# Moving the pooling mixer's PSUM bank to the pool of the wide products, and three empty steps in attention's turn, in a two-layer hybrid decoder trunk

## The chip, the cores and the metric

The kernel runs on one core of a Trainium2 chip, in float32 throughout; large matrix products are done with operands split into a high and a low part. The metric is the time of one execution on the device in microseconds, given as a median over runs.

## The reference

Two layers work on 256 positions of width 1024. In each layer, in this order:

```
h += 0.5 * SwiGLU(RMSNorm(h))                      # width 2816
u  = RMSNorm(h); one input projection of u, split into
     A) sparse attention: an indexer of 8 heads picks the 64 best keys of each query,
        8 heads attend to them through a latent of rank 256
     B) pooling mixer: means over trailing windows of 2, 4, 8, 16 minus the input,
        a 128x128 map for each of the 4 groups, a scale for each channel
     C) Mamba-2 state space: causal convolution, chunked scan in 2 chunks of 128,
        16 heads of 64 in 2 groups, SiLU gate, norm
     and three sigmoid gates
h += W_out( sum over branches of sigmoid(gate) * Lift(branch) )
h += 0.5 * SwiGLU(RMSNorm(h))
h += sigmoid(RMSNorm(h) W_g) * (p W_p)
```

A final RMSNorm follows the last layer. The change lies in the middle part, where A, B and C run beside one another.

## The kernel before, in words

**Products.** Activations lie transposed, 128 channels on the partitions and 256 positions along the free axis. A weight unit of 128x1024 is loaded, split by ScalarE into `whi` (line 140) and by VectorE into `wlo` (line 141), and used as the stationary operand. `mm3` (line 163) makes one product out of three: high by high (line 166), high by low (167), low by high (168). One pair of projection columns is 2 units x 8 blocks x 3 = 48 such products into one PSUM bank. They are called wide here: they use the whole 128x128 array.

**Narrow products.** Some products use half the array. Scores and indexer products have 64 contracted rows (`products`, line 684). Attention's values (`values`, line 765) and the state-space products within a chunk (`near`, line 927) have 64 output columns, one head. All of these go through `mm` (line 105), so all have line 106 in the profile; their tiles tell them apart: `aux<-ki,a` indexer, `aux<-a,a` scores, `aux<-t,a` values, `aux<-ct,ul` state space. Values and `near` are plain float32 and show two rows for a product.

**Banks.** PSUM is handed out by `bank` (line 92) from two pools of four banks: `mm` for the wide products, and `aux` for all that is small: narrow products, transposes (line 109), the state-space helpers and, at line 999, the pooling mixer's product.

**The weave.** After the projections that attention and the state space need, four generators run in turn (`weave`, line 645, called at line 602): `states` (the state space, weight 56), `attend` (attention, 34), `pools` (pooling, 24) and `gate` (the gate projections, 43). Each `yield` ends a step; the generator with the smallest share of steps done goes next. A step of `gate`, or of the projections in `pools`, issues 12 wide products. `states` and `attend` are `apart`: when one of them yields a function, it is parked until the other yields one too, and then the two functions are called one behind the other. So four times a layer a *round* is traced: `near` of one group and chunk, then attention's next products. The rounds are `near` with the scores of the first 128 queries; `near` with their values and the scores of four heads of the other queries; `near` with those values and the last scores; `near` with the last values.

**Order on TensorE.** The program is first traced and then ordered for each engine by a list scheduler that works with estimated times: an instruction traced earlier goes first among those that it takes to be ready. `mm` and `transpose` pin each of their instructions behind the TensorE instruction traced just before it; `mm3` doesn't, so wide products fill in wherever a narrow one isn't taken to be ready. The order on each engine is thus fixed when the kernel is built.

**Attention's chain.** `softmax` (line 731) masks and reduces each score on VectorE (line 744), takes the exponential on ScalarE (line 746), scales (line 750), transposes with TensorE (line 758) and copies out with ScalarE (line 761). It yields twice in the first part, three times to wait, and once behind each of two sets of transposes. `attention` (line 777) then yields once, and then hands over the function with the values.

**The pooling chain.** `pool_group` (line 975) copies its input out of PSUM (line 981), builds the window sums, splits the result (lines 185 and 186), and issues one `mm3` into the bank of line 999, which `split_scaled` (lines 189 and 190) reads.

Of the kernel before, what the change touches and what calls it, by code (L numbers as in the profile page):

```python
# [64 lines left out]
class Builder:  # L65
# [711 lines left out]
    def attention(self, mb, q, kt, vt, ya):  # L777


        two, pair, py = [], [], []  # L780

        def scores(h, g):
            two[:] = self.products(g, 4 // (h + 1), slice(h * P, (h + 1) * P), (h + 1) * P, q,
                                   lambda y, c: kt[y][:, c])

        def out(h):
            if not py:
                py.append(self.bank("aux"))
            self.values(h, py[0], pair, vt)
            pair.clear()  # L790

        def done(h):
            qs = slice(h * P, (h + 1) * P)
            self.split(ya[:, 0, :, qs], ya[:, 1, :, qs],
                       py.pop().rearrange("p (a b) -> p a b", a=4))

        yield lambda: scores(0, 0)
        yield from self.softmax(0, two, mb[0], pair)
        yield
        yield lambda: (out(0), scores(1, 0))  # L800
        done(0)
        yield from self.softmax(1, two, mb[1], pair)
        yield
        yield lambda: (out(1), scores(1, 2))
        yield from self.softmax(1, two, mb[1], pair)
        yield
        yield lambda: out(1)
        done(1)
# [166 lines left out]
    def pool_group(self, layer, g, ps, wpl, yp):  # L975
        nc = self.nc
        w = WINDOWS[g]
        pad = 16
        x = self.t([P, pad + S + 16], tag="t1")[:, :pad + S]
        nc.vector.memset(x[:, :pad], 0.0)  # L980
        nc.scalar.copy(x[:, pad:], ps)
        cur, have = x, 1
        while have < w:
            n = self.t([P, pad + S + 16], tag="t1")[:, :pad + S]
            nc.vector.tensor_copy(n[:, :have], cur[:, :have])
            nc.vector.tensor_tensor(n[:, have:], cur[:, have:], cur[:, :pad + S - have], op=OP.add)
            cur, have = n, 2 * have
        yield

        nc.vector.tensor_tensor(cur[:, pad:pad + 16], cur[:, pad:pad + 16],  # L990
                                self.col(layer, "pool_corr", g * 16, 16), op=OP.mult)
        y = self.t([P, S], tag="t1")
        nc.vector.scalar_tensor_tensor(y, cur[:, pad:], 1.0 / w, x[:, pad:],
                                       op0=OP.mult, op1=OP.subtract)
        yh = self.t([P, S], FR, tag="t1")
        yl = self.t([P, S], FR, tag="t1")
        self.split(yh, yl, y)
        yield
        po = self.bank("aux")
        s = slice(g * P, (g + 1) * P)  # L1000
        self.mm3(po[:, :S], (wpl[0][:, s], wpl[1][:, s]), (yh, yl), True, True)
        self.split_scaled(yp[:, 0, g], yp[:, 1, g], po[:, :S], self.col(layer, "pool_scale", g))
# [211 lines left out]
```

## Time and profile before

| what | value |
|---|---|
| median of 3 runs | 1325.61 us (1325.14 to 1326.77) |
| the profiled execution | 1326.89 us |
| its span, first to last instruction | 1325.2 us |
| mean granted clock of TensorE | 0.996 |
| layer 0: indexer, then the four rounds | 231.65, 259.18; 321.84, 337.97, 364.50, 381.80 us |
| layer 0: first product of the lift | 388.50 us |

PE is TensorE's products, PEld its loads of the stationary operand, DVE VectorE, ACT ScalarE. A row of the timeline gives the start and the duration in microseconds, the engine, the line, the operation, the tiles written and read, the part of the array used (rows*columns), the shape, and how many instructions the row merges. Products overlap: each takes about 0.28 us from its start to its modelled end, while the next one starts after about 0.11 us. What a product costs is therefore the distance between starts, and not its duration.

### The profile page before, as it was taken

The page shows a single profiled execution, that of the slowest core. Times are in us where ns is not written, and L with a number is a line of the kernel's source. Part 1 is how long each engine was busy: PE and PEld are TensorE (multiplying, and loading weights), DVE is VectorE, ACT ScalarE, POOL GpSimd, SP SyncE. Part 2 cuts the span into 40 slices and gives each one's busy share as a digit, 9 for nine tenths or more (in the row PEclk, how much of TensorE's full clock was granted, in tenths as well). Part 3 has the DMA queues.
Part 4 walks back from the last instruction along what each step waited for, and adds up shares of the span by engine and source line. Part 5 has one row for each costly group of instructions (what it writes and reads, how often), then busy time and mean ns, then how long its engine had stood idle before and what let it go on. Part 6 is the DMA issues. An engine that isn't in the chain of part 4 may idle for free.

```text
span 1325.2 us, 28279 instructions
## 1 busy us (share of the span) xinstructions
PE 1306.6 (99%) x11502; PEld 1296.1 (98%) x11502; DVE 1039.6 (78%) x1971; ACT 740.9 (56%) x1209; POOL 7.0 (1%) x17
## 2 busy tenths in 40 slices
PE   7999999999999999999999999999999999999997
PEld 7999999999999999999999999999999999999997
DVE  6877659987989787766887776699789888777666
ACT  5554446756864555444655444566577546544454
POOL 0000000000000000000000000000000000000000
PEclk9999999999999999999999999999999999999998
DMA  7666655567546566666656666556665466666661
GB/s 260 193 193 195 197 176 183 184 187 212 167 144 206 185 208 193 194 198 193 188 180 195 196 196 189 159 191 191 195 195 163 144 215 210 195 197 194 192 193 47
DMA packets 72385, 248.24 MB, mean 187 GB/s; under 512 B 7936, under 2 KB 10304, under 8 KB 72256
## 3 DMA queue, kind: packets, MB, share of 16 engines
q1 hardware_dynamic: 71392, 245.17, 60.2%
q8 instruction: 90, 1.47, 0.5%
q10 hardware_dynamic: 864, 1.28, 0.3%
q14 instruction: 39, 0.32, 0.1%
HBM read 245.33 MB, written 1.08 MB: 186 GB/s over the span
## 4 chain that ended last, share of the span: by engine, by line
PE 97%; DVE 1%; ACT 1%; DMA 0%; issue 0%; DVEq 0%; ACTq 0%
PE mm L166 30%; PE mm L168 30%; PE mm L167 30%; PE aux L106 3%; PE aux L167 1%; PE aux L168 1%; PE aux L166 1%; PE aux L109 1%; DMA h<-in_x_dram 0%; DVE wlo L141 0%; DVE acc L225 0%; ACT whi L140 0%; DVE ul L190 0%; ACT uh L189 0%; DVE h L1031 0%
## 5 line engine op out<-in xcount | busy, mean ns | idle before, releaser
L140 ACT CAST whi<-raw 128x1024 fp32r<-128x1024 f32 (+1 forms) x457 | 476.0, 1045 | 491.4 <-issue 229.1
L166 PE MATMUL mm<-uh,whi 128*128 128x256 f32 x2550 | 706.5, 279 | 7.2 <-ACT whi L160 6.7
L168 PE MATMUL mm<-uh,wlo 128*128 128x256 f32 x2560 | 708.9, 278 | 1.8 <-DVE wlo L141 1.8
L167 PE MATMUL mm<-ul,whi 128*128 128x256 f32 x2560 | 707.8, 277 | 0.0
L141 DVE TENSOR_TENSOR wlo<-raw,whi 128x1024 fp32r<-128x1024 f32 (+1 forms) x457 | 551.7, 1213 | 195.0 <-ACT whi L140 193.7
L166 PEld LDWEIGHTS mm<-uh,whi 128*128 128x128 f32 x2550 | 478.9, 188 | 9.8 <-ACT whi L160 6.7
L168 PEld LDWEIGHTS mm<-uh,wlo 128*128 128x128 f32 x2560 | 481.8, 188 | 3.0 <-DVE wlo L141 2.4
L167 PEld LDWEIGHTS mm<-ul,whi 128*128 128x128 f32 x2560 | 482.1, 188 | 0.2 <-DVE ul L190 0.2
L168 PE MATMUL mm<-gh,wlo 128*128 128x256 f32 x704 | 194.1, 276 | 0.0
L167 PE MATMUL mm<-gl,whi 128*128 128x256 f32 x704 | 194.1, 276 | 0.0
L166 PE MATMUL mm<-gh,whi 128*128 128x256 f32 x704 | 193.7, 276 | 0.0
L168 PEld LDWEIGHTS mm<-gh,wlo 128*128 128x128 f32 x704 | 132.2, 188 | 0.0
L167 PEld LDWEIGHTS mm<-gl,whi 128*128 128x128 f32 x704 | 132.2, 188 | 0.0
L166 PEld LDWEIGHTS mm<-gh,whi 128*128 128x128 f32 x704 | 131.9, 188 | 0.0
L167 PE MATMUL mm<-a,whi 128*128 128x256 f32 x256 | 70.3, 276 | 0.0
L166 PE MATMUL mm<-a,whi 128*128 128x256 f32 x256 | 70.2, 276 | 0.0
L168 PE MATMUL mm<-a,wlo 128*128 128x256 f32 x256 | 69.9, 277 | 0.0
L166 PEld LDWEIGHTS mm<-a,whi 128*128 128x128 f32 x256 | 47.9, 188 | 0.0
L167 PEld LDWEIGHTS mm<-a,whi 128*128 128x128 f32 x256 | 47.9, 188 | 0.0
L168 PEld LDWEIGHTS mm<-a,wlo 128*128 128x128 f32 x256 | 47.6, 188 | 0.0
L373 DVE TENSOR_TENSOR t<-mm,rs_r 128x256 f32<-128x256 f32 x88 | 37.2, 423 | 9.8 <-PE mm L168 0.6
L378 DVE SCALAR_TENSOR_TENSOR t<-t,t 128x256 f32<-128x256 f32 x88 | 37.4, 425 | 3.0
(215 smaller groups left out, 1105.7 us busy)
## 6 DMA issues: line engine op xcount, KB each, us to landing
raw<-in_w_dram SPq DMA_DIRECT2D x447, 512.0 KB, 4.3
gh<-rates SPq DMA_DIRECT2D x16, 256.0 KB, 4.3
raw<-in_w_dram SPq DMA_DIRECT2D x8, 352.0 KB, 3.0
raw<-in_w_dram SPq DMA_DIRECT2D x4, 256.0 KB, 3.7
gh<-rates SPq DMA_DIRECT2D x8, 128.0 KB, 3.4
h<-in_x_dram SPq DMA_DIRECT2D x2, 256.0 KB, 4.2
h<-in_x_dram SPq DMA_DIRECT2D x1, 512.0 KB, 5.7
t<-in_p_dram ACTq DMA_DIRECT2D x2, 256.0 KB, 5.9
```

The costliest lines, as they stand in the source:

```text
L106: self.tc.keep_in_program_order(self.nc.tensor.matmul(*args, **kw))
L109: self.tc.keep_in_program_order(self.nc.tensor.transpose(*args))
L140: nc.scalar.copy(hi[:, :n], raw[:, :n])
L141: ins = nc.vector.tensor_tensor(lo[:, :n], raw[:, :n], hi[:, :n].bitcast(F), op=OP.subtract)
L166: (self.mm if keep else mm)(ps, a[0], b[0], start=start, stop=False)
L167: mm(ps, a[0], b[1], start=False, stop=False)
L168: mm(ps, a[1], b[0], start=False, stop=stop)
L373: nc.vector.tensor_tensor(t, p1[0], r, op=OP.mult)
L378: nc.vector.scalar_tensor_tensor(g, th, 1.0, t, op0=OP.add, op1=OP.mult)
```

## The change

In `pool_group`, line 999, the bank for the product of each pooling group comes from the pool of the wide products. In `attention`, the generator yields once more ahead of each of the three functions that hold values (behind lines 799, 803 and 806). Nothing else differs: the same instructions, transfers and weight units. Every layer runs line 999 four times.

```
         yield lambda: scores(0, 0)
         yield from self.softmax(0, two, mb[0], pair)
         yield
+        yield
         yield lambda: (out(0), scores(1, 0))
         done(0)
         yield from self.softmax(1, two, mb[1], pair)
         yield
+        yield
         yield lambda: (out(1), scores(1, 2))
         yield from self.softmax(1, two, mb[1], pair)
+        yield
         yield
         yield lambda: out(1)
         done(1)
...
         yield
-        po = self.bank("aux")
+        po = self.bank()
         s = slice(g * P, (g + 1) * P)
         self.mm3(po[:, :S], (wpl[0][:, s], wpl[1][:, s]), (yh, yl), True, True)
```

In a few words it was described as one state-space bank from the pool of the wide products, and attention steps once more ahead of its values, so that narrow products lie in six runs a layer.

More of the change, by code (lines that the diff above doesn't have):

```diff
@@ L799, in attention @@
         yield
+        yield
         yield lambda: (out(0), scores(1, 0))
@@ L803, in attention @@
         yield
+        yield
         yield lambda: (out(1), scores(1, 2))
         yield from self.softmax(1, two, mb[1], pair)
+        yield
         yield
@@ L998, in pool_group @@
         yield
-        po = self.bank("aux")
+        po = self.bank()
         s = slice(g * P, (g + 1) * P)
```

## The prediction

> **What bounds the kernel now.** I read the page first, then who made TensorE wait, then the busy time of the stretch that the change touches, and last the order of TensorE's instructions in that stretch. From the page:
>
> ```profile
> span 1325.2 us, 28279 instructions
> PE 1306.6 (99%) x11502; PEld 1296.1 (98%) x11502; DVE 1039.6 (78%) x1971; ACT 740.9 (56%) x1209; POOL 7.0 (1%) x17
> PE 97%; DVE 1%; ACT 1%; DMA 0%; issue 0%; DVEq 0%; ACTq 0%
> ```
>
> The second line is busy time by engine, the third the chain that ended last. Both say TensorE. Its longest wait in the answer on waits is at the very start, and the busy time of 190 to 388 us, which holds all of layer 0's woven stretch, leaves it almost no gap:
>
> ```profile
> PE mm L166 <- ACT whi L160: 6.7, 1, 6.7
> 190.00:388.00 198.00, 197.79 (x1758) 193.23 (x1757) 172.58 (x389) 132.49 (x248) 2.37 (x2) 1.00 0.60 183
> ```
>
> TensorE is busy for 197.79 of 198.00 us there, at a granted clock of 1.00. So the change cannot gain by removing a wait of TensorE, for there is none; it can gain only if the same products take less of TensorE's time, and it loses by any wait that it puts in.
>
> How much time a product takes depends on its neighbours. Ordinary products use the whole array (128*128 in the rows). Narrow ones use half: 64 rows for scores, 64 columns for the state-space products and the attention values. The rows below are TensorE's timeline of layer 0 in order of start: start, duration, then the form and how many products the row merges. First the two runs of the indexer, with the wide products around one of them:
>
> ```profile
> 231.44 0.28 PE L168 MATMUL mm<-uh,wlo 128*128 128x256 f32 x1
> 231.65 1.55 PE L106 MATMUL aux<-ki,a 64*128 64x128 f32 x24
> 233.13 0.39 PE L166 MATMUL mm<-uh,whi 128*128 128x256 f32 x1
> 233.36 0.28 PE L167 MATMUL mm<-ul,whi 128*128 128x256 f32 x1
> ...
> 259.18 1.70 PE L106 MATMUL aux<-ki,a 64*128 64x256 f32 x24
> ```
>
> Then the four rounds in which the state-space products (ct,ul), the values (t,a) and the scores (a,a) are traced together:
>
> ```profile
> 321.84 1.09 PE L106 MATMUL aux<-ct,ul 128*64 128x128 f32 x16
> ...
> 337.97 0.65 PE L106 MATMUL aux<-ct,ul 128*64 128x128 f32 x6
> ...
> 338.98 0.87 PE L106 MATMUL aux<-ct,ul 128*64 128x128 f32 x10
> ...
> 340.12 0.28 PE L168 MATMUL mm<-uh,wlo 128*128 128x256 f32 x1
> 340.33 0.43 PE L106 MATMUL aux<-t,a 128*64 128x128 f32 x2
> 340.69 0.39 PE L166 MATMUL mm<-uh,whi 128*128 128x256 f32 x1
> 340.91 0.28 PE L167 MATMUL mm<-ul,whi 128*128 128x256 f32 x1
> 341.03 0.28 PE L168 MATMUL mm<-uh,wlo 128*128 128x256 f32 x1
> ...
> 342.30 1.09 PE L106 MATMUL aux<-t,a 128*64 128x128 f32 x14
> 343.31 0.38 PE L106 MATMUL aux<-a,a 64*128 64x256 f32 x1
> ...
> 344.69 0.28 PE L168 MATMUL mm<-uh,wlo 128*128 128x256 f32 x1
> 344.90 0.97 PE L106 MATMUL aux<-a,a 64*128 64x256 f32 x11
> 345.80 0.39 PE L166 MATMUL mm<-uh,whi 128*128 128x256 f32 x1
> 346.02 0.28 PE L167 MATMUL mm<-ul,whi 128*128 128x256 f32 x1
> ...
> 364.50 1.09 PE L106 MATMUL aux<-ct,ul 128*64 128x128 f32 x16
> 365.42 0.60 PE L106 MATMUL aux<-t,a 128*64 128x128 f32 x4
> ...
> 367.56 1.09 PE L106 MATMUL aux<-t,a 128*64 128x128 f32 x12
> ...
> 369.32 0.97 PE L106 MATMUL aux<-a,a 64*128 64x256 f32 x11
> ...
> 381.80 1.09 PE L106 MATMUL aux<-ct,ul 128*64 128x128 f32 x16
> 382.73 1.09 PE L106 MATMUL aux<-t,a 128*64 128x128 f32 x16
> ```
>
> Count the runs, a run being narrow products with no whole-array product between them. Indexer: two. Round one, at 321.84: one. Round two is torn into five (6 state-space products; 10 more; 2 values; 14 values and 1 score; 11 scores). Round three is torn into three (16 and 4; 12 and the first score; 11 scores). Round four: one. That is 12 a layer. Layer 1 is cut in the same places, as its row of 14 values shows:
>
> ```profile
> 993.28 1.09 PE L106 MATMUL aux<-t,a 128*64 128x128 f32 x14
> ```
>
> Six runs a layer would be the two of the indexer and one for each round, so the change says that it joins the five pieces of round two and the three of round three.
>
> **What one run costs.** Between two whole-array products of ordinary pace lies 0.12 us (340.91 to 341.03); 16 narrow ones take 0.92 us (364.50 to 365.42), 0.0575 each. The run of two at 340.33: from the wide product before it (340.12) to the second after it (340.91) pass 0.79 us. Two wide steps are 0.24 and two narrow ones 0.115, which leaves 0.435 us for going in and coming out. The run of 11 scores: from 344.69 to 346.02 pass 1.33 us, less 0.24 and 11 x 0.0575 = 0.63, leaves 0.46. The long indexer run: from 231.44 to 233.36 pass 1.92, less 0.24 and 24 x 0.0575 = 1.38, leaves 0.30. The two short runs are of the kind that would vanish, so I take 0.44 us and keep 0.30 and 0.46 as ends. The switch shows on both sides: 0.21 us from a wide product to the first narrow one, 0.22 between the first two wide ones after a run, where 0.12 is normal.
>
> The Trainium skill, TensorEngine Tiling (Array Packing), Key Properties, says that changing the tiling mode, and not merely the tile, drains TensorE. The trace agrees in kind: 0.435 and 0.46 us for a way in and a way out. The skill's TensorE: Matmul & The Clock Gate, Single matmul latency, puts a drain at about 175 ns; two of them, an estimate from that page, would be 0.35 us a run and 4.2 us for twelve.
>
> **The change part by part.** No instruction is added or taken away, no transfer, no weight unit; the order of the weight units stays too. What changes is which PSUM bank four small products a layer write, and where attention's steps fall between the others.
>
> *The bank (line 999).* The pooling mixer's product no longer takes one of the four "aux" banks, which near-products, values, scores and transposes share. In round two its product started at 337.76, straight before the state-space products at 337.97. With its bank, the state-space bank, the values' bank and the first score bank live, the four are full and the second score bank has to wait; by my reading that is why one score product runs at 343.31 and 11 follow only at 344.90. Round three ends in the same way, with 11 scores apart at 369.32. Without that tenant these two tears go. It also lets attention's transposes pass: in round three the second set is traced directly behind a pooling product and pinned to it. With the extra steps it is traced behind a gate product instead, though the first set then comes behind the pooling product.
>
> *The extra steps (after lines 799, 803, 806).* They hold the values back so that the softmax, the transposes and their copies are done when a round begins. Two values at 340.33 and 14 at 342.30 are parted by such a copy:
>
> ```profile
> 339.42 0.59 ACT L761 COPY t<-aux 128x512 f32<-128x512 f32 x1
> ```
>
> It ends at 340.01, and two values are already out at 340.33 with the first copy. Counting the code's steps, round two comes to stand behind no further wide product, rounds three and four each behind 24 more than now. Delay for the state-space branch, which waits parked for attention, is covered by those same gate products, so I cost it at nothing. If that cover were gone, the end would feel it: attention's result is ready at 385.17 and the lift begins at 388.50, so 3.3 us of cover are to spare, while 24 products less are 24 x 0.12 = 2.9 us.
>
> ```profile
> 384.48 0.69 DVE L186 TENSOR_TENSOR a<-aux,a 128x512 fp32r<-128x512 f32 x1 [0.72 <-ACT a L185]
> ...
> 388.50 0.28 PE L166 MATMUL mm<-a,whi 128*128 128x256 f32 x1
> ```
>
> *Sum.* Six runs fewer a layer, two layers: 12 x 0.44 = 5.3 us less on TensorE (ends 12 x 0.30 = 3.6 and 12 x 0.46 = 5.5). TensorE is the bound, so all of it comes off the end. The profiled execution took 1326.89 us, 1.7 more than its span and 1.3 above the median 1325.61; against it the sum is 1321.6, against the median 1320.3. The likeliest case's own range is 1319.5 to 1322.5: the two ends, with half a microsecond for the spread of the runs.
>
> **Rivals.** *Some tears stay.* Round two gets no wide product more ahead of it, and the copy at 339.42 still comes after the state-space products could start; values may again go out in two parts. If only the tears made by banks go, two to four runs a layer vanish: 4 x 0.44 = 1.8 to 8 x 0.44 = 3.5 us, 1322.1 to 1323.8. For it speaks that the tear between 2 and 14 values follows the copy and no bank.
>
> *The wide pool is asked in order, and TensorE stands.* This one ends slower. Banks of a pool seem to be granted in the order of the code: the state-space products of round two had their factors early (the multiply of line 922 ended at 330.38) and yet began only after the pooling product at 337.76, which asks for a bank before them. If the pool of the wide products does the same, the next pair of projections cannot start until the pooling product has its input:
>
> ```profile
> 329.09 1.29 DVE L922 TENSOR_TENSOR ct<-ct,gl 128x512 f32<-128x512 f32 x2
> ...
> 336.28 0.40 ACT L185 CAST t<-t 128x256 fp32r<-128x256 f32 x1
> ...
> 337.76 0.28 PE L166 MATMUL aux<-t,whi 128*128 128x256 f32 x1
> ...
> 359.37 0.41 ACT L185 CAST t<-t 128x256 fp32r<-128x256 f32 x1
> ...
> 362.26 0.28 PE L166 MATMUL aux<-t,whi 128*128 128x256 f32 x1
> ```
>
> The second pooling product stands in the code 48 wide products behind round one, and 24 more need no new bank. Round one begins at 321.84 and has 16 and 24 narrow products, 40 x 0.0575 = 2.3 us, so the 72 wide ones start at about 324.3 and are done 72 x 0.12 = 8.6 us later, at 332.9. The input is ready at 336.68, so TensorE would stand about 3.7 us. For the third pooling product the code's steps put 45 wide products fewer ahead of it than the trace has: 362.26 - 45 x 0.12 = 356.9, with the input ready at 359.78: 2.9 us, unless the first wait has swallowed it. Against 2.64 us saved by whole runs that is 1.1 to 4.0 us lost a layer: 1327.7 to 1333.5, say 1330.5. It decides wherever the pooling input comes later than the last product that has a bank already. Against it: the weave keeps two pairs going, and four banks hold both, one being emptied and one more. The Trainium skill, Perfetto Trace Analysis, Identifying Performance Opportunities, says that repeated gaps on the engine that should be full can mean too little PSUM for the next tile; here no such gap stands in the rows, and by that rule they would appear with the fifth tenant.
>
> *The change does not do what its words say*, and the order of the products stays as it is: 1325.6. The words speak of a state-space bank, while line 999 is the pooling mixer's; round two's unmoved place in the code speaks for a little of this, the two tears that a bank makes against it.
>
> **How the numbers follow.** A measurement of this kernel can tell about 0.2%, 2.65 us, from no change. Whole runs (1320.3) get 0.52, tears in part (1322.1 to 1323.8, half of it beyond 0.2%) 0.22, nothing 0.08, the standing TensorE 0.18. Faster: 0.52 + 0.11 = 0.63; within 0.2%: 0.11 + 0.08 = 0.19; slower 0.18. I name the likeliest, 1320.3. The range goes from 1319.5, under the full gain, to 1329.5, which takes in the smaller half of the slower case; what lies outside is about 0.14.
>
> **What would show it.** Right: TensorE's timeline has one narrow run in each round of both layers, no idle time before a pooling product, and the stretch from the first indexer run to the lift is 2.6 us shorter a layer, with all other stages as long as now. Tears in part: runs counted between 7 and 11. The standing TensorE: idle time on TensorE in the woven stretch, released by ScalarE's cast of line 185 or a release of a wide bank, where now there are 0.21 us. Wrong altogether: six runs and the stretch no shorter, which would mean that a run costs less than its neighbours' spacing says.

## The result, and the profile after

| kernel | median of 4 runs | lowest to highest | profiled execution | its span |
|---|---|---|---|---|
| before | 1325.41 us | 1325.14 to 1326.77 | 1326.89 us | 1325.2 us |
| after | 1339.47 us | 1338.98 to 1340.77 | 1339.73 us | 1338.0 us |

The change makes the kernel slower: the ratio is 1.0103, with a 95% interval of 1.0091 to 1.0116, or 14.1 us. The forecast was 1320.3 us. (The profiled execution of before lies 1.5 us above its median, so the two profiles differ by 12.8 us in span.)

The page of the changed kernel, its span, its busy times and its chain:

```profile
span 1338.0 us, 28291 instructions
...
PE 1306.5 (98%) x11502; PEld 1296.9 (97%) x11502; DVE 1044.9 (78%) x1971; ACT 741.8 (55%) x1209; POOL 7.0 (1%) x17
...
PE 90%; DVE 5%; ACT 3%; issue 1%; DMA 1%; DVEq 0%; SPq 0%; ACTq 0%
```

TensorE is busy for 1306.5 us, against 1306.6 before, with the same 11502 products. The span is 12.8 us longer, so TensorE idles 1338.0 - 1306.5 = 31.5 us where it idled 18.6: 12.9 us more. The chain says the same in another way: TensorE's share fell from 97% to 90%, and VectorE and ScalarE now hold 8% of it. The answer on waits names the place (the columns are: us in total, times, the longest):

```profile
PE mm L166 <- ACT t L185: 10.9, 4, 4.8
PE mm L166 <- ACT whi L160: 6.8, 1, 6.8
PE aux L109 <- ACT t L750: 2.1, 2, 1.0
```

The first and the third line are new: 10.9 + 2.1 = 13.0 us, the whole growth of the idle time. Line 166 with the bank `mm` and an input from the cast of line 185 is the pooling product, which waits for its input. Now TensorE's timeline of layer 0, from before round two to the end of round three (a bracket gives the idle time before the row and what ended it):

```profile
327.07 0.39 PE L166 MATMUL mm<-t,whi 128*128 128x256 f32 x1 [0.62 <-ACT t L185]
...
333.00 0.60 PE L109 MATMUL aux<-ident,t 128*128 128x128 f32 x4
334.64 1.21 PE L109 MATMUL aux<-ident,t 128*128 128x128 f32 x4 [1.04 <-ACT t L750]
335.81 0.39 PE L166 MATMUL mm<-t,whi 128*128 128x256 f32 x1
...
338.90 0.28 PE L168 MATMUL mm<-uh,wlo 128*128 128x256 f32 x1
339.11 1.09 PE L106 MATMUL aux<-ct,ul 128*64 128x128 f32 x16
340.03 1.04 PE L106 MATMUL aux<-t,a 128*64 128x128 f32 x16
341.01 0.98 PE L106 MATMUL aux<-a,a 64*128 64x256 f32 x12
341.92 0.39 PE L166 MATMUL mm<-uh,whi 128*128 128x256 f32 x1
342.14 0.28 PE L167 MATMUL mm<-ul,whi 128*128 128x256 f32 x1
...
356.49 0.28 PE L168 MATMUL mm<-uh,wlo 128*128 128x256 f32 x1
361.59 0.58 PE L166 MATMUL mm<-t,whi 128*128 128x256 f32 x1 [4.83 <-ACT t L185]
361.97 0.41 PE L166 MATMUL mm<-uh,whi 128*128 128x256 f32 x1
362.19 0.41 PE L167 MATMUL mm<-ul,whi 128*128 128x256 f32 x1
...
370.38 1.09 PE L106 MATMUL aux<-ct,ul 128*64 128x128 f32 x16
371.31 1.09 PE L106 MATMUL aux<-t,a 128*64 128x128 f32 x16
372.33 0.98 PE L106 MATMUL aux<-a,a 64*128 64x256 f32 x12
```

Three things are to be seen. First, the narrow products lie as the change's words say, in six runs a layer, though the bank that moved is the pooling mixer's and not one of the state space: rounds two and three are one run each (16 state-space products, 16 values, 12 scores, with no wide product between), and the two layers together have 12 runs where they had 24. From 338.90 to 342.14 pass 3.24 us, less two wide steps of 0.12 leaves 3.0 for the whole of round two, and 3.1 for round three. The five and three pieces of before, measured in the same way, took 4.9 and 4.2 us. (Round three of before stands directly behind four transposes, whose own steps are not counted; here are the rows ahead of it.)

```profile
363.85 0.28 PE L168 MATMUL aux<-t,wlo 128*128 128x256 f32 x1
363.97 0.60 PE L109 MATMUL aux<-ident,t 128*128 128x128 f32 x4
```

That saves 3.1 us a layer, 0.52 for each run that vanished.

Second, TensorE stands before the pooling products: 0.62 us before the first; 2.81 us (333.00 to 335.81) with only eight transposes in them before the second; 4.83 us before the third. The next pair of projections, which had its inputs, follows each time only behind the pooling product. Third, the wide products behind the longest wait start 0.21 us apart (361.97 to 362.19 and on) and not 0.12. The busy times of that wait and of the stretch behind it show why; the number behind PE, PEld, DVE, ACT and POOL is the granted clock:

```profile
356.00:361.60 5.60, 0.77 (x8) 0.57 (x7) 5.13 (x13) 2.90 (x7) 0.00 (x0) 0.94 0.62 200
361.60:366.40 4.80, 4.80 (x22) 4.80 (x23) 3.48 (x13) 0.62 (x2) 0.00 (x0) 0.50 0.35 119
```

The granted clock is 0.50 over these 4.80 us, in which 22 products start; at the step of 0.113 us that wide products have elsewhere, 42 would. None of this counts as idle time, and so it hides in the busy time that did not fall. From 361.97, 21 products take 4.48 us instead of 21 x 0.113 = 2.4, a loss of 2.1 us; in layer 1, where the same wait of 4.83 us stands, the same 21 lose 1.4 us. In layer 0 the clock is still low behind them: the next two wide products and eight transposes take 1.65 us, and in layer 1, with the clock back, 1.03, which is 0.6 us more.

The account of the two layers: +13.0 us idle (6.49 in each), +4.1 at half clock, some +1.7 around the transposes (2.81 us a layer, less 1.04 that counts as idle and 8 x 0.115, the step of a wide product, for the transposes), -6.2 for whole runs: +12.6 us. From the first indexer product to the lift, layer 0 grew from 156.85 to 164.32 us and layer 1 from 156.79 to 162.96, 13.6 us together. (That is more than the 12.8 us between the spans, because the profiled execution of before reached its first indexer product 0.9 us later.) The remaining 1.0 us I did not place.

### The profile page after: what moved, and what is told of

Its sections match the earlier page's. It is cut to its first block, busy times and chain, and to the rows that moved or that the text cites. A ratio compares the mean times of both kernels' runs of the same rounds, so it can differ in the third digit from the quotient of the medians.

```text
span 1338.0 us, 28291 instructions
## 1 busy us (share of the span) xinstructions
PE 1306.5 (98%) x11502; PEld 1296.9 (97%) x11502; DVE 1044.9 (78%) x1971; ACT 741.8 (55%) x1209; POOL 7.0 (1%) x17
## 4 chain that ended last, share of the span: by engine, by line
PE 90%; DVE 5%; ACT 3%; issue 1%; DMA 1%; DVEq 0%; SPq 0%; ACTq 0%
PE mm L166 28%; PE mm L168 28%; PE mm L167 28%; PE aux L106 2%; DVE wlo L141 2%; ACT whi L140 1%; PE aux L109 1%; ACT t L746 1%; PE aux L167 1%; DVE ct L919 1%; PE aux L168 1%; PE aux L166 1%; DVE acc L225 0%; DMA h<-in_x_dram 0%; DMA raw<-in_w_dram 0%
```

## The experiments

The first theory, A: the banks of a pool are granted in the order of the code, so that a pooling product that asks the pool `mm` for a bank and has no input yet holds up every later pair of projections, ready or not. Theory B: the extra steps make attention late, and its banks and results hold up the rest. Theory C: the pool `mm` has too few banks with a fifth tenant. Each experiment was timed in five rounds beside the kernel before, on the same chip (medians of before 1325.45 for the first four, 1325.44 for the others). Runs are counted in TensorE's timeline, over both layers; idle is the span less TensorE's busy time.

| kernel | runs | idle, us | median, us | ratio (95%) |
|---|---|---|---|---|
| before | 24 | 18.6 | 1325.4 | |
| after | 12 | 31.5 | 1339.47 | 1.0103 (1.0091 to 1.0116) |
| bank alone | 16 | 30.4 | 1341.13 | 1.0115 (1.0101 to 1.0129) |
| steps alone | 26 | 18.2 | 1327.95 | 1.0019 (1.0010 to 1.0028) |
| early first write | 34 | 18.6 | 1329.94 | 1.0034 (1.0021 to 1.0046) |
| indexer torn | 36 | 18.9 | 1331.29 | 1.0047 (1.0033 to 1.0061) |
| wait filled | 14 | 21.2 | 1337.18 | 1.0086 (1.0072 to 1.0100) |
| input's bank, more steps | 12 | 19.9 | 1321.39 | 0.9971 (0.9961 to 0.9982) |
| input's bank, three steps | 22 | 19.8 | 1326.75 | 1.0009 (1.0000 to 1.0018) |
| asked one step later | 16 | 24.5 | 1327.65 | 1.0016 (1.0007 to 1.0025) |

### The bank alone, and the steps alone

The change's two halves, one by one. The bank alone:

```
-        po = self.bank("aux")
+        po = self.bank()
```

> The bank of line 999 from the wide pool, without the extra steps. Its order on TensorE has 16 narrow runs in all (24 before, 12 after). Theory A (the wide pool grants its banks in the order of the code, so the next pair of projections stands behind a pooling product whose input is late): the waits for the cast of line 185 stay, one of 4 to 5 us and one of about 0.6 us a layer, and the time is 1338 to 1342 us. Theory B (the extra steps make attention and the parked state-space branch late): no such wait, and 8 runs fewer than before at 0.58 us each, 1321 us. Theory C (too few wide banks, whatever the order of asking): as A.

The steps alone:

```
         yield from self.softmax(0, two, mb[0], pair)
         yield
+        yield
         yield lambda: (out(0), scores(1, 0))
...
         yield
+        yield
         yield lambda: (out(1), scores(1, 2))
         yield from self.softmax(1, two, mb[1], pair)
+        yield
         yield
         yield lambda: out(1)
```

> The three extra steps, with the pooling product in the small pool as before. 26 narrow runs. Theory A and theory C: TensorE has no wait in the woven stretch, and two runs more than before cost about 1 us: 1326 to 1327 us. Theory B: waits of several us a layer, about 1339 us.

The bank alone took 1341.13 us, 15.7 more than before, and TensorE's waits are those of the changed kernel:

```profile
PE mm L166 <- ACT t L185: 9.9, 4, 4.3
PE mm L166 <- ACT whi L160: 6.6, 1, 6.6
PE aux L109 <- ACT t L750: 2.0, 2, 1.1
```

The steps alone took 1327.95 us, 2.5 more, with no wait on a cast of line 185 in its answer on waits. So the loss belongs to the bank, and B falls. The steps by themselves do not make the runs whole either: there are 26, two more than before.

### An early first write

The changed kernel, with one product more into each pooling bank, in a half that nothing reads, whose operands are there long before. Its result is not used. The bank is asked for at the same place and kept as long; only its first write no longer waits for the pooling input.

```
         po = self.bank()
+        nc.tensor.matmul(po[:, S:], self.onesr, wpl[0][:, :S], start=True, stop=True)
```

> The changed kernel with one more product for each pooling group, whose result nobody reads: it writes the unused half of the group's bank from operands that are ready early, so that the bank is asked for and granted at once. Eight products more in all (1 us), 34 narrow runs. Theory A: the waits for the cast of line 185 go, since the next pair no longer stands behind the late input; 10 runs more than before cost about 5 us and the products 1 us: 1330 to 1332 us. Theory B: the waits stay, 1339 us or more. Theory C: the waits stay too, since the bank is held longer than in the changed kernel: 1339 us or more.

It took 1329.94 us, 9.5 less than the changed kernel, with eight products more. All that its answer on TensorE's waits holds:

```profile
PE mm L166 <- ACT whi L160: 6.3, 1, 6.3
PE mm L168 <- DVE wlo L141: 1.3, 3, 0.9
PE mm L166 <- ACT whi L140: 1.1, 1, 1.1
PE aux L106 <- DVE acc L225: 1.0, 1, 1.0
PE aux L106 <- ACT t L223: 0.8, 1, 0.8
```

The waits for line 185 and for the transposes are gone, with the same four banks and the same five tenants. Too few banks cannot be the cause, and C falls; what held TensorE up was the order in which the banks are first written. The prediction's sentence from the Trainium skill, Perfetto Trace Analysis, Identifying Performance Opportunities, that such gaps can mean too little PSUM, named a sign that came, but not its cause here. A second finding came unasked: without the wait there are 34 runs. So the changed kernel's whole runs seem to be owed in part to the standing itself: with nothing wide ready, nothing could come between. (Every edit here also lets the list scheduler order TensorE anew, so no run changes the banks and nothing else.)

### The indexer torn

What a run costs: the kernel before, with the two runs of the indexer in each layer cut into eight, and the four rounds as they were.

```
-        self.weave((choose(), 26), (silus(), 60), (some(12), 12))
+        self.weave((choose(), 34), (silus(), 60), (some(12), 12))
...
+    def product_steps(self, g, per, qs, nk, q, key, sides):
+        sides += [(self.bank("aux"), *self.heads(g + i, per)) for i in range(2)]
         for j in range(per):
             for x, y in ((0, 0), (1, 0), (0, 1)):
...
+            yield
...
+        all_sides = []
+        for g in range(0, 8 // per, 2):
+            yield from self.product_steps(g, per, qs, nk, qi, lambda y, c: ki[y], all_sides)
```

> The kernel before, with the indexer's two runs a layer cut into eight by a step after each six products; everything else in TensorE's order is as before, with 36 runs instead of 24. It prices a run by itself. At the 0.44 us of the prediction 12 more runs give 1330.7 us; at the 0.30 us of the long indexer run 1329.0; at the 0.58 us by which rounds two and three became shorter in the changed kernel, 1332.4; if only neighbours shift and nothing is lost, 1325.4.

It took 1331.29 us, 5.84 more. But the edit does more than the expectation says. For the second 128 queries `product_steps` is called twice with the same growing list, so its second call issues the products of the first call again: 12 more a layer, 24 in all. TensorE's count shows them (11526 against 11502), and so do the indexer's runs, of which two in each layer have 12 products and not 6:

```profile
PE 1310.6 (99%) x11526; PEld 1297.4 (98%) x11526; DVE 1039.7 (78%) x1971; ACT 741.4 (56%) x1209; POOL 3.4 (0%) x17
263.06 0.98 PE L106 MATMUL aux<-ki,a 64*128 64x256 f32 x12
```

A run of 24 such products takes 1.70 us in the kernel before (at 259.18), a run of 12 here 0.98, so one costs 0.060 us and the 24 cost, as an estimate, 1.4 us. That leaves 4.4 us for 12 runs more, 0.37 us a run. The early first write bears this out: 10 runs more and eight wide products (0.9 us), with as much idle time as before, cost 4.5 us, which is 0.36 a run. The 0.58 us in the expectation counted transposes of the kernel before as part of round three; it should be the 0.52 us above.

### The wait filled

The changed kernel, with 48 products more in each layer ahead of the third pooling product, into an `aux` bank that nothing reads. It asks what the half clock costs.

```
+        if g == 2:
+            pd = self.bank("aux")
+            for _ in range(48):
+                nc.tensor.matmul(pd[:, :S], self.onesr, wpl[0][:, :S], start=True, stop=True)
         po = self.bank()
```

> The changed kernel with 48 products more a layer, whose results nobody reads, in a bank of the small pool just ahead of the third pooling product: TensorE has them to do where it now waits 4.83 us. 48 x 0.113 = 5.4 us of work fills the wait; 14 narrow runs instead of 12. If the halved granted clock behind that wait comes from the wait, it stays at 1.00 and the 2.1 + 0.7 us of layer 0 and the 1.4 us of layer 1 that the slow products cost are won back: 1339.5 - 4.2 + 0.8 (work longer than the wait) + 1.0 (two runs) = 1337 us, with 96 products more. If the clock falls for another reason, 1341 us.

With 96 products more the kernel took 1337.18 us, 2.3 less than the changed one. The same moment of layer 0, its busy times with the granted clock as above:

```profile
358.00:362.00 4.00, 4.00 (x36) 4.00 (x35) 3.41 (x13) 0.77 (x3) 0.00 (x0) 1.00 0.64 205
362.00:366.00 4.00, 4.00 (x37) 4.00 (x37) 3.04 (x8) 3.19 (x7) 0.00 (x0) 1.00 0.18 24
```

The clock stays at 1.00, and there is no wait of 4.8 us left. So the half clock follows from the wait, and its price comes on top of it.

### Asked one step later

The changed kernel, with one more step between the split of the pooling input and the asking for the bank:

```
         self.split(yh, yl, y)
         yield
+        yield
         po = self.bank()
```

> The changed kernel with one step more in the pooling group between the split of its input and the asking for the wide bank. 16 narrow runs. Theory A: the third product is asked for after round three, when its input has long been ready, so the wait of 4.83 us and the halved clock go; the small waits in round two may stay (0.6 us and the transposes in a block, some 3 us a layer): 1325.4 - 8 x 0.49 + 2 x (1 to 3) = 1323.5 to 1327.5 us. Theory C (number of banks, not the order): about 1339 us.

It took 1327.65 us, 11.8 less than the changed kernel, with the same bank from the same pool. Its waits:

```profile
PE mm L166 <- ACT t L185: 3.5, 4, 1.1
...
PE aux L109 <- ACT t L750: 2.1, 2, 1.0
```

The wait for line 185 went from 10.9 to 3.5 us, though only the place of the asking in the code moved. The sum comes near: 8 runs fewer than before are 8 x 0.37 = 3.0 us saved, and 24.5 - 18.6 = 5.9 us more idle; +2.9, and +2.2 were measured.

### The bank of its own input

If the order of asking is the trouble, a pooling product that asks for no bank has none. Here it is written into the half bank from which its own input was copied, which it holds anyway:

```
-        po = self.bank("aux")
         s = slice(g * P, (g + 1) * P)
-        self.mm3(po[:, :S], (wpl[0][:, s], wpl[1][:, s]), (yh, yl), True, True)
+        self.mm3(ps, (wpl[0][:, s], wpl[1][:, s]), (yh, yl), True, True)
```

with the read by `split_scaled` changed likewise. One kernel has the change's three steps. In the other there are two extra ahead of the first values, four ahead of the second and none ahead of the third, chosen so that the order on TensorE has six runs a layer.

> The pooling product in its input's bank, and just the three extra steps of the change. 22 narrow runs. Theory A: no wait, two runs fewer than before: 1324.5 us. The difference to the changed kernel, about 15 us, is then due to the bank alone. Theory B: about 1339 us.

> The pooling product goes into the half bank from which its own input was copied out, so it asks for no bank at all; two extra steps ahead of the first values, four ahead of the second, none ahead of the third. 12 narrow runs, as in the changed kernel. Theory A: no wait of TensorE in the woven stretch, and 12 runs fewer at the 0.49 us of the torn indexer give 1319.6 us (1318.4 at 0.58). Theory B (late values cost the time): six extra steps a layer, slower than the changed kernel's three, over 1339 us. Theory C (too few wide banks): the input's bank is held longer, some waits, 1325 us or more.

With the change's steps it took 1326.75 us, with no wait for line 185 on a pooling product, and 22 runs. Against the changed kernel that is 12.7 us less, with the same steps and ten runs more: the bank's price, net of the runs that it made whole. With the other steps it took 1321.39 us, 4.05 less than the kernel before (interval of the ratio 0.9961 to 0.9982), the only version faster than both. Its waits:

```profile
PE mm L168 <- DVE wlo L141: 1.8, 5, 0.9
...
PE mm L166 <- ACT t L185: 0.9, 2, 0.5
```

It has the 12 runs that the change was described with, and 1.3 us more idle than before. 12 x 0.37 = 4.4 saved, less 1.3, makes 3.1; 4.05 were measured. The expectations, 1319.6 and 1324.5 us, were each some 2 us too low: they left out these small waits, and the first counted 12 runs at 0.49 us.

The input's bank with three steps, with two runs fewer and 1.2 us more idle, should be +0.5 and is +1.3. For these two and the kernel that asks later, the sum of runs and idle time is thus right to about 1 us. For the steps alone it is not: they should cost 2 x 0.37 - 0.4 = 0.3 us and cost 2.5. What the rest is stays open.

## Why the prediction was wrong

**What bounds the kernel: right.** TensorE was full, and a change could lose by any wait that it puts in. That happened.

**The whole runs: right in number and near in price, but in part by luck.** Six runs a layer came, as announced. A run was put at 0.44 us with ends of 0.30 and 0.46; the torn indexer says 0.37, rounds two and three 0.52. With 0.37 the sum would have been 4.4 us, with 0.52 6.2, and not 5.3. The forecast's only gain was thus there, in about the size that it said. The tears put down to the banks did go: the 12 scores are together in rounds two and three of all seven kernels whose pooling product has left the small pool, and apart, as 1 and 11, in the three that keep it there. The other tear of round two, 2 values and 14, went for another reason than the extra steps. With the steps and no long wait (the input's bank, three steps) it is still there, among 22 runs; with the bank alone and no steps round two is whole. What joined it in the changed kernel seems to be the standing of TensorE, which the forecast did not count on.

**The bank (line 999): the step that failed.** It counted what the bank's departure gives to the small products and put nothing on its arrival in the pool of the wide ones; that went to a rival with a chance of 0.18. The sentence that kept the rival small was "four banks hold both, one being emptied and one more". It counts banks. The runs showed that the count does not matter (early write, the same banks: no wait), but the place of the asking (one step later: 10.9 us of waits become 3.5) and that there is an asking at all (the input's bank: none of these waits with three steps, 0.9 us with more). A hint was in the prediction already: the state-space products with early factors that began only behind the pooling product (that the bank was the reason there, no run tested). In the pool `mm` it was the bound that was held up.

**The rival's places were right, its price was too low.** It put the end of the wide products ahead of the second pooling product at 332.9; the trace has 333.00. It put the third at 356.9; the last wide product ahead of it starts at 356.49. At the second, it said a wait of 3.7 us; the input was ready somewhat earlier, and eight transposes lay in the gap, so about 1.9 us were lost (2.81 - 0.9). At the third it said 2.9 us and 4.83 came, because it took the input's time from the trace of before. ScalarE's casts of the changed kernel:

```profile
335.37 0.39 ACT L185 CAST t<-t 128x256 fp32r<-128x256 f32 x1
...
361.14 0.40 ACT L185 CAST t<-t 128x256 fp32r<-128x256 f32 x1 [2.70 <-DVE t L996]
```

The third cast ends at 361.54, where it ended at 359.78. It waits for VectorE, whose window sums (lines 988 to 996, which are 985 to 993 before) have weight splits (line 141) among them:

```profile
354.55 0.42 DVE L989 TENSOR_TENSOR t<-t 128x271 f32<-128x271 f32 x1
...
355.30 1.21 DVE L141 TENSOR_TENSOR wlo<-raw,whi 128x1024 fp32r<-128x1024 f32 x1
...
357.25 1.21 DVE L141 TENSOR_TENSOR wlo<-raw,whi 128x1024 fp32r<-128x1024 f32 x1
...
359.14 1.21 DVE L141 TENSOR_TENSOR wlo<-raw,whi 128x1024 fp32r<-128x1024 f32 x1
...
360.69 0.41 DVE L996 SCALAR_TENSOR_TENSOR t<-t,t 128x256 f32<-128x256 f32 x1
```

Three splits of 1.21 us lie between the first sum and line 996. Before there were two, and the sums, which began a tenth of a microsecond earlier, came to the same line at 358.92 and not at 360.69:

```profile
355.35 1.22 DVE L141 TENSOR_TENSOR wlo<-raw,whi 128x1024 fp32r<-128x1024 f32 x1
...
357.79 1.21 DVE L141 TENSOR_TENSOR wlo<-raw,whi 128x1024 fp32r<-128x1024 f32 x1
358.92 0.41 DVE L993 SCALAR_TENSOR_TENSOR t<-t,t 128x256 f32<-128x256 f32 x1
```

While TensorE stood, VectorE split weights, and the one thing that TensorE needed was queued behind. Two more terms were missing from the rival: the first pooling product's 0.62 us, and the half clock, 2.7 and 1.4 us. Worked out with what was measured: 2 x (0.62 + 1.9 + 4.83) for the three waits, 4.1 for the clock, less 6.2 for whole runs, is 12.6 us more than before, 1338.0 us; that is most of the measured 14.1.

**The extra steps: nothing to the wait, as said.** They were costed at nothing, and with the steps alone there is no new wait for line 185. They cost 2.5 us by themselves, of which two runs more explain 0.7. That they would make the runs whole failed: by themselves they leave 26.

**What would show it** named idle time released by the cast of line 185 as the mark of the standing TensorE, and the first line of the waits after is just that.

## What to carry to other kernels

When a buffer is moved to another pool, look not only at how many buffers that pool has, but at who asks for them in which order and when each asker can first write: one late writer in the queue of a full engine's pool holds up all the ready ones behind it. A tenant with late inputs goes to a buffer that it holds already, or asks as late as the code allows. Take the time of such a wait not from the trace of before alone, since the engines that feed it are given other work while the full engine stands, and add what the engine's clock takes to come back.

## What the runs showed of the hardware

**The clock fell behind every wait of 4.3 to 4.8 us in the woven stretch, and at times behind a shorter one.** After 4.83 us without a product the granted clock was 0.50 over 4.8 us in layer 0 and 0.60 on average over the 1.7 us behind them; in layer 1 it was 0.60 on average over 4.1 us. With the bank alone it was 0.50 over 3.8 us behind waits of 4.35 and 4.34 us. Around the waits of 0.62 and 1.04 us of the changed kernel it stays at 1.00 (327.00 to 332.00 and 334.60 to 339.00; the third row is layer 1 behind the long wait):

```profile
327.00:332.00 5.00, 4.92 (x43) 4.93 (x44) 4.96 (x24) 5.00 (x21) 0.00 (x0) 1.00 0.52 153
334.60:339.00 4.40, 4.36 (x31) 3.71 (x31) 4.18 (x9) 4.30 (x10) 0.00 (x0) 1.00 0.45 143
...
1019.80:1023.90 4.10, 4.09 (x22) 4.09 (x23) 3.37 (x13) 0.64 (x2) 0.00 (x0) 0.60 0.42 148
```

So the long wait costs its own 4.8 us and 1.4 to 2.7 more. The Trainium skill, TensorE: Matmul & The Clock Gate, Part 1: The HAM clock gate, says that an idle window of about 3.4 us halves the clock and a busy one of that length gives it back, in windows that run freely. The rows agree with that in the long waits, and the two layers lost different amounts behind equal ones. But the clock also fell behind less idle time than such a window. Near the start of the kernel before, TensorE waits 0.46 us, runs two products, and waits 1.41 us:

```profile
14.32 0.58 PE L168 MATMUL mm<-uh,wlo 128*128 128x256 f32 x1 [1.41 <-DVE wlo L141]
```

From 14.5 to 17.5 us the granted clock is 0.50. At the same place it falls in two more of the ten profiled executions, both of the input's bank (0.50 and 0.56, behind waits of 0.7 to 0.9 us), and stays at 1.00 in seven, one of which (the early first write) has waits of 1.13 and 0.92 us there. So waits of about 1 us can be enough and need not be; what decides it, no run here shows.

**Going in and out of a narrow run costs about 0.37 us** by the torn indexer and 0.36 by the early first write, within the 0.30 to 0.46 that the neighbours' spacing showed. The joined rounds saved 0.52 for each; why more, no run here shows.
